# Far weight rooms moved by 64 bytes, and two short groups of small bfloat16 products in a tuned two-block transformer kernel

## The chip, the cores and the metric

The kernel runs on one core of a Trainium2 chip. The core has five engines that run their own instruction lists side by side: TensorE (PE, matrix products; its weight loads are listed apart as PEld), VectorE (DVE), ScalarE (ACT), GpSimd (POOL) and SyncE (SP, which here issues the DMAs). They share the on-chip memory SBUF; products land in PSUM. The metric is the time of one execution on the device in microseconds (us); lower is better. Three runs of the kernel before gave 1571.7, 1567.13 and 1571.4 us, median 1571.4.

## The reference

Two transformer blocks run one after the other on 256 tokens of width 1024, all in float32.

```python
# block 1
h = rms_norm(x, g_norm1) * (1 + scale1) + shift1
z = h @ w_in                                   # attention, index heads, pooling, gates
mixed = (g_attn * y_attn + g_pool * y_pool) @ w_out
x = x + gate1 * mixed
h2 = rms_norm(x, g_norm2) * (1 + scale2) + shift2
# experts: 16384 rows in u and v; 8 heads choose 16 each
s = einsum(h2 @ w_q, sub_keys); top_k twice     -> expert, gate
act = gelu(einsum('nd,ned->ne', h2, u[expert]))
x = x + gate2 * einsum('ne,ned->nd', gate * act, v[expert])
# block 2: recurrence and sparse attention, then the feed-forward
up = causal_dwconv(rms_norm(x, norm2_g) @ w_up, ffn_conv_w, ffn_conv_b)
gate, val = split(up, 2)
x = x + (gelu(gate) * val) @ w_down
```

The kernel does not gather the chosen experts. It multiplies with all of u (128 units), multiplies the result with a gate that is zero for experts that were not chosen, and multiplies that with all of v (128 units).

## The kernel before

**Units.** All large weights come as units of 128 partitions by 1024 float32 (8 blocks of 128x128). A unit is loaded by SP into `raw` (L116). ACT copies it rounded to `wh` (L178), and DVE, or POOL for some units of u, forms the rest `wl` = raw - wh (L179). The activations are split the same way (`h2` and its like: a high and a low part). `mm3` (L202) then multiplies a unit: 8 blocks wh x high, 8 blocks wh x low, 8 blocks wl x high, so 24 matmuls, each of 128x128 weights (a weight load of its own) against 256 columns. They add up in one PSUM tile `mm`.

**Rooms.** A unit's wh and wl lie in a room. The list `plan` (L152) says which units go to which rooms, repeating a string of letters. "w" are the two near rooms of pool `wp`, on the left of SBUF. "b" are two rooms in the tile `wpx` (L360) of pool `hot`, on the right; they serve w1 from unit 8, wup1 and wout1. "c" are two rooms of pool `wpu`, on the right, and serve u from unit 2 to 60 in the string "wwcc" (two units near, two far). "d" are three rooms in `spare` for v from unit 64, "e" one more near room from w2 on. The pool `hot` also holds, one after the other, the activations (`hot_acts`, L80: h2 for the experts, hb for w2) and the split gate products `pr` (L850). So in a matmul of u the moving activation lies in `hot` on the right, and the weight in a near or a far room.

**Order.** PE runs the units in the order of the code: w1, wup1, wout1, wpq (the queries of the experts), the first half of u (units 0 to 63, L825), the second half of u (L844) with 32 gate batches between its units, v (L869), w2, wup2, wout2, the feed-forward's first product (wff: 48 units in 24 steps `m` of two units) and second product (wdn: 24 units). During the first half of u, DVE works through the choice of the experts (`topk`, a generator of which a piece runs after most units). A gate batch (`gate_batch`, L784) builds masks on DVE and then runs 16 bfloat16 matmuls of 128x64 (L810) into a PSUM tile with the tag "x".

**Feed-forward.** For every step m (L1438) and i = 0, 1: a unit of wff, DVE scales the product to `zf` (L1445), ACT starts the convolution `cc` (L1448), DVE adds its two other taps (L1450, two instructions). After both: ACT applies gelu, POOL multiplies the halves (L1454), ACT rounds the product to `ffh` (L223), and DVE forms `ffl` (L224). The second product takes all 24 of ffh and ffl as moving operand: for each of 8 output tiles three units, of which the third needs ffh and ffl 16 to 23 (L1456).

`identb` is a bfloat16 unit matrix of 128x128, made at the start.

Of the kernel before, what the change touches and what calls it, by code (L numbers as in the profile page):

```python
# [7 lines left out]
F32 = mybir.dt.float32  # L8
F32R = mybir.dt.float32r
# [49 lines left out]
def tile_kernel(ctx: ExitStack, tc: tile.TileContext, I, out):  # L59
    nc = tc.nc  # L60
    V, S, G, T = nc.vector, nc.scalar, nc.gpsimd, nc.tensor
# [9 lines left out]
    px = ctx.enter_context(tc.tile_pool(name="px", bufs=2, space=PSUM))  # L71

    def pool(stack, name, bufs=1, **kw):
        return stack.enter_context(tc.tile_pool(name=name, bufs=bufs, reuse_waits="tile", **kw))
# [3 lines left out]
    hot = ctx.enter_context(tc.tile_pool(name="hot", bufs=1, reuse_waits="tile", side="right"))  # L78

    def hot_acts(name):  # L80
        t = hot.tile([128, 2, 8, 256], F32R, name=name, tag="hot")
        return t[:, 0], t[:, 1]


# [2 lines left out]
    x = const.tile([128, 8, 256], F32, name="x", tag="x")  # L87
# [16 lines left out]
    identb = const.tile([128, 128], BF, name="identb")  # L104
# [78 lines left out]
    def weights(name, i):  # L183

        if not ready:
            now[0] = None
            prefetch()
        now[0] = ready.pop(0)
        assert stream[now[0].pos] == (name, i)
        u = now[0]  # L190
        while len(ready) < 4 and prefetch():
            pass
        return u

    def mm3(ps, blocks, start=True, stop=True, by_block=False):

# [153 lines left out]
    with ExitStack() as ph:  # L350
# [6 lines left out]
        stp = ExitStack()  # L357
        psu = pool(stp, "psu", space=PSUM)
        wps = pool(stp, "wps", 6, side="left")
        wpx = hot.tile([128, 2, 2, 8, 128], F32R, name="wpx", tag="hot")  # L360
        rooms["a"] = Room(6, wps)
        rooms["b"] = Room(2, pairs=[(wpx[:, n, 0], wpx[:, n, 1]) for n in range(2)])
        sqrt_next()
# [3 lines left out]
        for i in range(2):  # L367
            pc = px.tile([128, 4, 128], F32, name="pc", tag="x")
            for k in range(4):
                T.matmul(pc[:, k], ident[0:8, 4 * i + k:4 * i + k + 1].to_broadcast([8, 128]), c8,  # L370
                         start=True, stop=True)
# [7 lines left out]
        h = (b1h.tile([128, 8, 258], F32R, name="hh"), b1h.tile([128, 8, 258], F32R, name="hl"))  # L379
# [16 lines left out]
        for m in range(8):  # L396
# [7 lines left out]
            n = b1w.tile([128, 256], F32, name="hn", bufs=3)  # L404
# [105 lines left out]
        for b in range(2):  # L510
            nk = 128 * (b + 1)
            sl = slice(b * 128, (b + 1) * 128)
            for gg in range(2):
                P = b1w.tile([128, 2, 2, 256], F32, name="P1")
                mx = b1w.tile([128, 3, 2, 2], F32, name="mx", bufs=3)
                for s in range(2):
                    base = 64 * s
                    pl = pa.tile([128, 2, 256], F32, name="pl", tag="a")
                    for c in range(2):
# [5 lines left out]
                        else:  # L525
                            tc.add_manual_dep(mm.ins, first.ins.name, no_sync(), reason="bank start")
                    T.matmul(pl[:, :, :nk], identb, bias[b][:, None, :].to_broadcast([128, 2, nk]),
                             start=False, stop=True, skip_group_check=True)
# [16 lines left out]
                for c in range(2):  # L545
                    po = px.tile([128, 128], F32, name="po", tag="x")
                    for s in range(2):
                        for k in range(b + 1):
                            T.matmul(po[64 * s:64 * s + 64], vt[:, k], pT[:, k, s, c],
                                     start=(k == 0), stop=(k == b))  # L550
# [106 lines left out]
        pxu = pool(upst, "pxu", 2, space=PSUM)  # L657
# [22 lines left out]
        for hd in range(8):  # L680
# [9 lines left out]
            for k in (2 * hd - 2, 2 * hd - 1) if 1 <= hd <= 4 else ():  # L690
                n = scr.tile([128, 256], F32, name="hn", bufs=2)
# [131 lines left out]
        rst = ExitStack()  # L823
        actA = None
        for i in range(64):  # L825
            if i == 0:
                pactA = pool(rst, "pactA", side="right")
                actA = [(0, pA0.tile([128, 24, 256], F32, name="actA0", tag="A0")),
                        (24, pactA.tile([128, 40, 256], F32, name="actA1"))]
                ust = ExitStack()  # L830
                rooms["c"] = Room(2, pool(ust, "wpu", 2, side="right"))
            u_unit(i, actA)
            if i == 0:
                late()
            if i % 5:
                next(tk, None)
# [10 lines left out]
                gate_batch(0, actA, n0, pxu if n0 % 16 else px)  # L847
                n0 += 8
        upst.close()
        pv_ = hot.tile([128, 8, 2, 256], F32R, name="pr", tag="hot")  # L850
        prs = [(pv_[:, 2 * n], pv_[:, 2 * n + 1]) for n in range(3)]
        vst = ExitStack()
        pv = pool(vst, "pv", side="right", space=PSUM)
# [15 lines left out]
        for i in range(128):  # L869
            u = weights("v", i)  # L870
            if i % 2 == 0:
                src = row(actA if i < 64 else actB, i % 64, 2)
                pr = prs[i // 2 % 3]
# [71 lines left out]
    with ExitStack() as ph:  # L945
# [131 lines left out]
        for kv in range(2):  # L1077
# [20 lines left out]
            for hf in range(2):  # L1098
                for l in range(8):
                    T.matmul(phd, cw[hf][:, l], cb[:, 8 * hf + l], start=(hf == 0 and l == 0),  # L1100
                             stop=(hf == 1 and l == 7))
# [332 lines left out]
    with ExitStack() as ph:  # L1434
        f1 = pool(ph, "f1", side="right")
        fw = pool(ph, "fw", 2, side="right")
        ff = (f1.tile([128, 24, 256], F32R, name="ffh"), f1.tile([128, 24, 256], F32R, name="ffl"))
        for m in range(24):  # L1438
            cv = []
            for i in range(2):  # L1440
                u = weights("wff", 2 * m + i)
                ps = pm4.tile([128, 256], F32, name="mm")
                mm3(ps, [(u, k, hf_, k) for k in range(8)], by_block=m == 0)
                z = fw.tile([128, 256], F32, name="zf", bufs=4)
                V.tensor_tensor(z, ps, r4, OP.mult)  # L1445
                ch = 24 * i + m
                cc = fw.tile([128, 256], F32, name=f"cc{i}")
                S.activation(cc, z, AF.Identity, bias=vcol("fb", ch), scale=vcol("fw", 96 + ch))  # L1448
                for j, d in ((1, 1), (0, 2)):
                    V.scalar_tensor_tensor(cc[:, d:], z[:, :256 - d], vcol("fw", 48 * j + ch),  # L1450
                                           cc[:, d:], op0=OP.mult, op1=OP.add)
                cv.append(cc)
            fact(cv[0], cv[0], AF.Gelu_apprx_tanh)
            G.tensor_tensor(cv[0], cv[0], cv[1], OP.mult)  # L1454
            split_act(ff, m, cv[0])
        for m in range(8):  # L1456
            ps = pm4.tile([128, 256], F32, name="mm")
            for j in range(3):
                u = weights("wdn", 3 * m + j)
                mm3(ps, [(u, k, ff, 8 * j + k) for k in range(8)], start=(j == 0), stop=(j == 2))  # L1460
            V.tensor_tensor(x2[:, m], ps, x2[:, m], OP.add)
            nc.sync.dma_start(out[:, m], x2[:, m])
# [112 lines left out]
```

## Time and profile before

| | |
|---|---|
| runs | 1571.7, 1567.13, 1571.4 us; median 1571.4 |
| profiled execution | 1572.43 us, of which the profile's span 1570.0 us |
| mean granted clock of TensorE | 0.989 of full speed |
| PE matmuls, busy | 1514.9 us (96%), 11758 matmuls |
| DVE, busy | 1286.6 us (82%) |
| ACT, busy | 831.3 us (53%) |
| POOL, busy | 213.6 us (14%) |
| HBM traffic | 279 MB read, 179 GB/s over the span |

The stages of the profiled execution, by the time at which PE works on them (us from the start of the span): w1, wup1, wout1 and wpq 57 to 217; first half of u 217 to 419; second half of u 419 to 609; v 610 to 980; w2 981 to 1277; wup2 and wout2 1277 to 1362; wff 1362 to 1499; wdn 1499 to 1567.

How to read it: matmuls of PE overlap. One that is listed with 0.28 us starts some 0.115 us after the one before it, so the pace is read from the starts, not from the durations. A row with "x16" stands for 16 instructions in a row of the same kind, its time running from the first start to the last end.

### The profile page before, as it was taken

The numbers are of one execution on the slowest core, as the hardware profiler recorded it, in microseconds if no ns is written. First come the engines' busy times: TensorE is split into PE (matmuls) and PEld (weight loads), VectorE is DVE, ScalarE is ACT, GpSimd is POOL, SyncE is SP. The second block draws the span as 40 slices with busy tenths as digits, with TensorE's granted clock in tenths as the row PEclk, the third lists the DMA queues.
The fourth block names the chain that finished last, engine by engine and source line by source line (L and its number), as shares of the span: only waits on it lengthen the run. The fifth ranks groups of instructions, "written<-read, shape, count | busy, mean of one in ns | idle before, by whom it ended". The sixth has DMA issues, their size and how long they took to land. (4 is left out here: it accounts for less than half of the span.)

```text
span 1570.0 us, 29771 instructions
## 1 busy us (share of the span) xinstructions
PE 1514.9 (96%) x11758; PEld 1404.7 (89%) x11758; DVE 1286.6 (82%) x2439; ACT 831.3 (53%) x1453; POOL 213.6 (14%) x156
## 2 busy tenths in 40 slices
PE   4999998999999999999999999988999999999999
PEld 3989998998999998888888888988888889999999
DVE  8899899993788987999966666978977766899963
ACT  3556564444444445444444444656777664666642
POOL 0100136896000000000000000026000000111100
PEclk9999999999999999999999999989999999999999
DMA  8778544655455555555566667453433235555663
GB/s 306 256 247 290 170 146 144 198 176 182 158 173 175 174 175 175 175 175 168 186 217 220 214 205 265 154 164 126 138 104 110 85 120 177 183 186 187 188 202 117
DMA packets 78203, 282.99 MB, mean 180 GB/s; under 512 B 8680, under 2 KB 9968, under 8 KB 77808
## 3 DMA queue, kind: packets, MB, share of 16 engines
q1 hardware_dynamic: 78064, 281.10, 54.8%
q8 instruction: 92, 1.51, 0.4%
q14 instruction: 47, 0.39, 0.1%
HBM read 278.97 MB, written 2.10 MB: 179 GB/s over the span
## 5 line engine op out<-in xcount | busy, mean ns | idle before, releaser
L178 ACT ACTIVATE wh<-raw 128x1024 fp32r<-128x1024 f32 x389 | 411.4, 1059 | 421.0 <-PE mm L202 212.8
L179 DVE TENSOR_TENSOR wl<-raw,wh 128x1024 fp32r<-128x1024 f32 x339 | 427.6, 1262 | 92.3 <-ACT wh L178 90.5
L202 PE MATMUL mm<-h,wh 128*128 128x256 f32 x2048 | 263.8, 282 | 0.0
L202 PEld LDWEIGHTS mm<-h,wh 128*128 128x128 f32 x2048 | 249.5, 191 | 0.2
L865 PE MATMUL vo<-spare,pr 128*128 128x512 f32 x768 | 176.0, 391 | 0.0
L865 PEld LDWEIGHTS vo<-spare,pr 128*128 128x128 f32 x768 | 144.2, 188 | 31.6
L202 PE MATMUL mm<-h,wl 128*128 128x256 f32 x1024 | 141.9, 282 | 8.3 <-DVE wl L179 8.3
L179 POOL TENSOR_TENSOR wl<-raw,wh 128x1024 fp32r<-128x1024 f32 x50 | 136.5, 2753 | 69.8 <-ACT wh L178 32.6
L268 POOL TENSOR_TENSOR r<-r,sq 128x256 f32<-128x256 f32 x18 | 13.7, 762 | 952.6 <-DVE hb L281 586.8
L202 PEld LDWEIGHTS mm<-h,wl 128*128 128x128 f32 x1024 | 129.9, 192 | 8.9 <-DVE wl L179 8.9
L202 PE MATMUL mm<-hb,wh 128*128 128x256 f32 x928 | 130.7, 287 | 0.6 <-ACT wh L178 0.2
L865 PE MATMUL vo<-wh,pr 128*128 128x512 f32 x512 | 130.8, 397 | 0.3 <-ACT pr L874 0.3
L179 DVE TENSOR_TENSOR spare<-raw,spare 128x1024 fp32r<-128x1024 f32 x64 | 78.4, 1226 | 56.3 <-ACT spare L178 56.0
L202 PEld LDWEIGHTS mm<-hb,wh 128*128 128x128 f32 x928 | 117.6, 192 | 3.7 <-issue 1.4
L178 ACT ACTIVATE spare<-raw 128x1024 fp32r<-128x1024 f32 x64 | 67.8, 1060 | 86.5 <-PE vo L865 85.8
L865 PEld LDWEIGHTS vo<-wh,pr 128*128 128x128 f32 x512 | 93.7, 188 | 19.0 <-ACT pr L874 0.4
L202 PE MATMUL mm<-hb,wl 128*128 128x256 f32 x464 | 69.3, 282 | 0.0
L865 PE MATMUL vo<-wl,pr 128*128 128x512 f32 x256 | 69.2, 392 | 0.0
L299 DVE SCALAR_TENSOR_TENSOR raw<-raw,cb 128x1024 f32<-128x1024 f32 x48 | 58.2, 1218 | 7.8 <-DMA raw<-in_wada_dram 7.8
L202 PEld LDWEIGHTS mm<-hb,wl 128*128 128x128 f32 x464 | 60.2, 190 | 0.3
L865 PEld LDWEIGHTS vo<-wl,pr 128*128 128x128 f32 x256 | 48.1, 188 | 10.7
L202 PE MATMUL mm<-hfh,wh 128*128 128x256 f32 x384 | 55.5, 281 | 0.0
(435 smaller groups left out, 2796.8 us busy)
## 6 DMA issues: line engine op xcount, KB each, us to landing
raw<-in_u_dram SPq DMA_DIRECT2D x128, 512.0 KB, 3.6
raw<-in_v_dram SPq DMA_DIRECT2D x128, 512.0 KB, 3.7
raw<-in_w_dram SPq DMA_DIRECT2D x86, 512.0 KB, 4.2
raw<-in_wada_dram SPq DMA_DIRECT2D x48, 512.0 KB, 5.2
raw<-in_wff_dram SPq DMA_DIRECT2D x48, 512.0 KB, 3.6
raw<-in_wup_dram SPq DMA_DIRECT2D x27, 512.0 KB, 3.9
raw<-in_wdn_dram SPq DMA_DIRECT2D x24, 512.0 KB, 3.5
raw<-in_wout_dram SPq DMA_DIRECT2D x16, 512.0 KB, 4.2
```

Source lines behind the costliest of these rows:

```text
L178: S.activation(u.h, t, AF.Copy)
L179: (G if n in on_pool and on_pool[n](i) else V).tensor_tensor(u.l, t, u.h.bitcast(F32), OP.subtract)
L202: T.matmul(ps, (u.l if wl else u.h)[:, s], a[al][:, k], start=start and n == 0, stop=stop and n == len(seq) - 1)
L268: eng.tensor_tensor(tot, tot, sq, OP.add)
L299: V.scalar_tensor_tensor(t, t, 1.0, cb, op0=OP.mult, op1=OP.mult, accum_out=a)
L865: T.matmul(vo[b][hf], pr[al][:, i % 2, b * 128:b * 128 + 128], (u.l if wl else u.h)[:, 4 * hf:4 * hf + 4], start=(i == 0 and n == 0), stop ...
```

## The change

It has two parts.

The first moves addresses. Every tile of the pool `hot` becomes 4128 instead of 4096 float32 long (128 bytes more in each partition; the added part is not used), the rooms "b" in `wpx` begin 16 floats (64 bytes) into their tile, and a tile of 16 floats (64 bytes) is put ahead of the rooms "c". What lies behind `hot` on the right moves by 128 bytes. The distance in bytes between a weight's address and its activation's, as the program lays the tiles out, is thus:

| weight room, stages | before, modulo 128 | after, modulo 128 | before, modulo 512 | after, modulo 512 |
|---|---|---|---|---|
| near rooms, u, w2, wout2, wff, wdn | 64 | 64 | 320 | 448 |
| far rooms "c", u 2 to 60 | 0 | 64 | 0 | 448 |
| rooms "b", wup1 and wout1 | 0 | 64 | 128 | 192 |
| near rooms, wup1 and wout1 | 64 | 64 | 448 | 64 |

The second part adds `pause(psum)`: 16 bfloat16 matmuls of identb (128x128) against 64 columns of identb, each with a weight load of its own, into a PSUM tile of the tag "x" that nobody reads. It stands in two places: ahead of unit 2 of u, and in the feed-forward ahead of the first unit of step m = 1.

```diff
@@ -78,7 +78,8 @@
     hot = ctx.enter_context(tc.tile_pool(name="hot", bufs=1, reuse_waits="tile", side="right"))
 
     def hot_acts(name):
-        t = hot.tile([128, 2, 8, 256], F32R, name=name, tag="hot")
+        t = hot.tile([128, 4128], F32R, name=name, tag="hot")[:, 0:4096].rearrange(
+            "p (h k n) -> p h k n", h=2, k=8)
         return t[:, 0], t[:, 1]
 
 
@@ -191,6 +192,12 @@
         while len(ready) < 4 and prefetch():
             pass
         return u
+
+    def pause(psum):
+
+        t = psum.tile([128, 8, 64], F32, name="pause", tag="x")
+        for n in range(16):
+            T.matmul(t[:, n % 8], identb, identb[:, 0:64], start=True, stop=True)
 
     def mm3(ps, blocks, start=True, stop=True, by_block=False):
 
@@ -357,7 +364,8 @@
         stp = ExitStack()
         psu = pool(stp, "psu", space=PSUM)
         wps = pool(stp, "wps", 6, side="left")
-        wpx = hot.tile([128, 2, 2, 8, 128], F32R, name="wpx", tag="hot")
+        wpx = hot.tile([128, 4128], F32R, name="wpx", tag="hot")[:, 16:4112].rearrange(
+            "p (n h k f) -> p n h k f", n=2, h=2, k=8)
         rooms["a"] = Room(6, wps)
         rooms["b"] = Room(2, pairs=[(wpx[:, n, 0], wpx[:, n, 1]) for n in range(2)])
         sqrt_next()
@@ -823,11 +831,14 @@
         rst = ExitStack()
         actA = None
         for i in range(64):
+            if i == 2:
+                pause(pxu)
             if i == 0:
                 pactA = pool(rst, "pactA", side="right")
                 actA = [(0, pA0.tile([128, 24, 256], F32, name="actA0", tag="A0")),
                         (24, pactA.tile([128, 40, 256], F32, name="actA1"))]
                 ust = ExitStack()
+                pool(ust, "wpu_pad", side="right").tile([128, 16], F32, name="wpu_pad")
                 rooms["c"] = Room(2, pool(ust, "wpu", 2, side="right"))
             u_unit(i, actA)
             if i == 0:
@@ -847,7 +858,8 @@
                 gate_batch(0, actA, n0, pxu if n0 % 16 else px)
                 n0 += 8
         upst.close()
-        pv_ = hot.tile([128, 8, 2, 256], F32R, name="pr", tag="hot")
+        pv_ = hot.tile([128, 4128], F32R, name="pr", tag="hot")[:, 0:4096].rearrange(
+            "p (m i n) -> p m i n", m=8, i=2)
         prs = [(pv_[:, 2 * n], pv_[:, 2 * n + 1]) for n in range(3)]
         vst = ExitStack()
         pv = pool(vst, "pv", side="right", space=PSUM)
@@ -1439,6 +1451,8 @@
             cv = []
             for i in range(2):
                 u = weights("wff", 2 * m + i)
+                if m == 1 and i == 0:
+                    pause(px)
                 ps = pm4.tile([128, 256], F32, name="mm")
                 mm3(ps, [(u, k, hf_, k) for k in range(8)], by_block=m == 0)
                 z = fw.tile([128, 256], F32, name="zf", bufs=4)
```

On DVE, ACT, POOL and SP the order of instructions is that of before; on PE it differs by the two pauses.

**First place**, PE before unit 2 of u. (`mm_...` are the PSUM tiles of one unit each, `h2` the activations of the experts, `pq` the scores of the chosen queries.) Before:

```order
L675 MATMUL pq_2759<-sub_2305,qh_2699 128x128 [waits Activation_49]
L675 MATMUL pq_2759<-sub_2305,qh_2699 128x128
L202 MATMUL mm_2764<-h2_2304,wh_2668 128x256 [waits DVE_49,PE_49]
L202 MATMUL mm_2764<-h2_2304,wh_2668 128x256 x15
L202 MATMUL mm_2764<-h2_2304,wl_2669 128x256 [waits Pool_49]
L202 MATMUL mm_2764<-h2_2304,wl_2669 128x256 x7
L202 MATMUL mm_2822<-h2_2304,wh_2724 128x256 [waits DVE_49]
L202 MATMUL mm_2822<-h2_2304,wh_2724 128x256 x15
L202 MATMUL mm_2822<-h2_2304,wl_2725 128x256 [waits Pool_49]
```

Before, the next unit follows at once. After, one pair of a weight load and a small matmul is shown, and 15 more like it are left out:

```order
L683 MATMUL pq_2763<-sub_2305,qh_2699 128x128
L209 MATMUL mm_2768<-h2_2304,wh_2668 128x256 [waits DVE_49,PE_49]
L209 MATMUL mm_2768<-h2_2304,wh_2668 128x256 x15
L209 MATMUL mm_2768<-h2_2304,wl_2669 128x256 [waits Pool_49]
L209 MATMUL mm_2768<-h2_2304,wl_2669 128x256 x7
L200 LDWEIGHTS identb_95
L200 MATMUL pause_2808<-identb_95 128x64
...
L209 MATMUL mm_2843<-h2_2304,wh_2728 128x256 [waits DVE_49]
L209 MATMUL mm_2843<-h2_2304,wh_2728 128x256 x15
L209 MATMUL mm_2843<-h2_2304,wl_2729 128x256 [waits Pool_49]
```

The 16 pairs of a weight load and a small matmul stand between unit 1 and unit 2, with no wait of their own; the units' own waits on DVE and POOL stay.

**Second place**, PE in the feed-forward between the two units of step 0 (by blocks, so wh, wl and both activation parts change from matmul to matmul) and the first unit of step 1. Before:

```order
L202 MATMUL mm_15965<-hfh_15610,wh_15869 128x256
L202 MATMUL mm_15965<-hfl_15611,wh_15869 128x256
L202 MATMUL mm_15965<-hfh_15610,wl_15870 128x256
L202 MATMUL mm_16006<-hfh_15610,wh_15924 128x256 x8
L202 MATMUL mm_16006<-hfl_15611,wh_15924 128x256 x8
L202 MATMUL mm_16006<-hfh_15610,wl_15925 128x256 x8
L202 MATMUL mm_16043<-hfh_15610,wh_15961 128x256 [waits Activation_49]
L202 MATMUL mm_16043<-hfh_15610,wh_15961 128x256 x7
```

Before, the row of units goes on into step 1 at its fourth row. After, again with one pair shown of 16:

```order
L209 MATMUL mm_15987<-hfh_15632,wh_15891 128x256
L209 MATMUL mm_15987<-hfl_15633,wh_15891 128x256
L209 MATMUL mm_15987<-hfh_15632,wl_15892 128x256
L200 LDWEIGHTS identb_95
L200 MATMUL pause_16028<-identb_95 128x64 [waits PE_49]
...
L209 MATMUL mm_16045<-hfh_15632,wh_15946 128x256 x8
L209 MATMUL mm_16045<-hfl_15633,wh_15946 128x256 x8
L209 MATMUL mm_16045<-hfh_15632,wl_15947 128x256 x8
L209 MATMUL mm_16082<-hfh_15632,wh_15983 128x256 [waits Activation_49]
L209 MATMUL mm_16082<-hfh_15632,wh_15983 128x256 x7
```

The pairs stand ahead of the first unit of step 1; the first of them waits for earlier work of PE itself on its PSUM tile.

## Rows read from the trace of the kernel before

**Rows 1.** The page: busy time, share of span and instructions of each engine.

```profile
PE 1514.9 (96%) x11758; PEld 1404.7 (89%) x11758; DVE 1286.6 (82%) x2439; ACT 831.3 (53%) x1453; POOL 213.6 (14%) x156
```

**Rows 2.** Windows: stretch, length, busy us by engine (instructions), PE clock, DMA share, GB/s.

```profile
130.00:160.00 30.00, 30.00 (x255) 30.00 (x254) 29.74 (x60) 16.51 (x26) 0.00 (x0) 1.00 0.84 293
217.00:360.00 143.00, 133.52 (x1095) 132.26 (x1094) 141.74 (x407) 64.09 (x104) 112.23 (x40) 0.97 0.49 159
360.00:419.00 59.00, 59.00 (x492) 59.00 (x492) 24.86 (x43) 28.21 (x43) 21.85 (x9) 0.98 0.58 188
419.00:609.00 190.00, 190.00 (x2027) 188.86 (x2026) 166.32 (x287) 83.87 (x127) 0.00 (x0) 1.00 0.54 175
1400.00:1490.00 90.00, 90.00 (x767) 90.00 (x766) 88.86 (x145) 60.59 (x97) 11.80 (x16) 1.00 0.60 188
1499.00:1530.00 31.00, 31.00 (x265) 31.00 (x264) 16.49 (x19) 12.78 (x15) 1.79 (x1) 1.00 0.64 200
```

**Rows 3.** Timeline of PE: start us, us, instructions; far units, then wout2.

```profile
231.84 2.08 PE L202 MATMUL mm<-h,wh 128*128 128x256 f32 x16
234.72 2.08 PE L202 MATMUL mm<-h,wh 128*128 128x256 f32 x16
...
1345.63 1.98 PE L202 MATMUL mm<-mix,wh 128*128 128x256 f32 x16
1348.36 1.98 PE L202 MATMUL mm<-mix,wh 128*128 128x256 f32 x16
```

**Rows 4.** Timeline of PE around one gate batch in the second half of u.

```profile
428.55 0.64 PE L810 MATMUL gt<-ab 128*128 128x64 f16 x16
429.03 2.08 PE L202 MATMUL mm<-h,wh 128*128 128x256 f32 x16
430.94 1.07 PE L202 MATMUL mm<-h,wl 128*128 128x256 f32 x8
431.85 1.98 PE L202 MATMUL mm<-h,wh 128*128 128x256 f32 x16
```

**Rows 5.** Waits between 217 and 420 us: total us, times, longest.

```profile
PE mm L202 <- DVE wl L179: 8.3, 3, 4.1
```

**Rows 6.** Timeline at the second of these waits, DVE and PE.

```profile
355.86 3.40 DVE L179 TENSOR_TENSOR wl<-raw,wh 128x1024 fp32r<-128x1024 f32 x1
...
359.31 2.08 PE L202 MATMUL mm<-h,wl 128*128 128x256 f32 x8 [3.74 <-DVE wl L179]
```

**Rows 7.** Windows right behind that wait, columns as in rows 2.

```profile
359.20:362.20 3.00, 2.89 (x13) 2.89 (x14) 0.06 (x1) 0.00 (x0) 0.00 (x0) 0.50 0.65 179
362.20:366.00 3.80, 3.80 (x34) 3.80 (x33) 1.23 (x1) 2.57 (x4) 0.67 (x1) 0.98 1.00 400
```

**Rows 8.** Timeline of PE early in wff, step m = 0.

```profile
1364.36 0.70 PE L273 MATMUL ss<-r,ones 128*128 128x256 f32 x2 [0.54 <-POOL r L268]
```

**Rows 9.** DVE between 1400 and 1490 us by line: count, busy us, mean ns, idle before.

```profile
L179 DVE TENSOR_TENSOR wl<-raw,wh 128x1024 fp32r<-128x1024 f32 x32 | 47.2, 1477 | 0.0
L1450 DVE SCALAR_TENSOR_TENSOR cc<-zf,vec,cc 128x255 f32<-128x255 f32 x33 | 15.7, 475 | 0.0
L1450 DVE SCALAR_TENSOR_TENSOR cc<-zf,vec,cc 128x254 f32<-128x254 f32 x32 | 15.5, 483 | 1.1
L1445 DVE TENSOR_TENSOR zf<-mm,r 128x256 f32<-128x256 f32 x32 | 13.4, 418 | 0.0
L224 DVE TENSOR_TENSOR ffl<-cc,ffh 128x256 fp32r<-128x256 f32 x16 | 6.6, 412 | 0.0
```

**Rows 10.** Timeline where wff ends and wdn begins.

```profile
1499.74 1.11 PE L202 MATMUL mm<-ffl,wh 128*128 128x256 f32 x8
...
1503.83 0.42 ACT L223 ACTIVATE ffh<-cc 128x256 fp32r<-128x256 f32 x1 [1.89 <-POOL cc L1454]
1504.28 0.42 DVE L224 TENSOR_TENSOR ffl<-cc,ffh 128x256 fp32r<-128x256 f32 x1 [1.08 <-ACT ffh L223]
...
1504.46 1.10 PE L202 MATMUL mm<-ffh,wh 128*128 128x256 f32 x8
```

## The prediction

> **What bounds the kernel now.** I read the page's engine totals first: PE is busy for 1514.9 of 1570.0 us, DVE for 1286.6 [rows 1]. A share over the whole span says little, so the second view is the windows by stage [rows 2]. The reader should see three kinds of stage there. In the second half of u, and from 360 to 419, PE is busy all the time and DVE is not: what a matmul takes is what the stage takes. In the first half of u up to 360, DVE has 141.74 of 143 us and PE waits. In the first product of the feed-forward both are full: 90.00 and 88.86 of 90 us.
>
> The third view is the timeline of PE, read for starts. The same instruction, 128x256 float32, runs at three paces. A unit of 24 in a far room takes 234.72 - 231.84 = 2.88 us, 120 ns each; a unit of wout2 takes 1348.36 - 1345.63 = 2.73 us, 113.5 ns each [rows 3]; in the feed-forward 40 matmuls take 1504.46 - 1499.74 = 4.72 us, 118 ns each [rows 10]. I call them 120, 118 and 113. At full clock all three occur, so the clock is not the reason. Two things go with the pace. One is the room: far rooms, where the distance of weight and activation is 0 modulo 128 bytes, are at 120 throughout. The other is history: near rooms keep 113 or 118 for hundreds of matmuls and change when something breaks the row of units. A gate batch of 16 small matmuls is such a break. It takes 429.03 - 428.55 = 0.48 us, the next 16 matmuls take 1.91 us instead of 1.81, and then 8 take 0.91, which is 113 [rows 4]. The whole second half of u has 32 batches and 2027 - 32 x 16 = 1515 large matmuls in 190.0 us: (190.0 - 32 x 0.58) / 1515 = 113.2 [rows 2]. In the feed-forward the pace falls to 118 behind a short wait at 1364 [rows 8], and 118 it stays.
>
> The Trainium skill speaks against a part of this. Its page "TensorE: Matmul & The Clock Gate", "Step-by-step: what each phase is for", says that PE has two independent read ports into SBUF and that loading the next weights takes no bandwidth from the running matmul. By that, an address could not matter, and moving the rooms would be worth nothing. The trace does not agree: 2.88 against 2.73 us for the same 24 matmuls at full clock.
>
> **Pauses, their own price.** By the gate batch one pause is 0.48 + 0.10 = 0.58 us of PE. It copies the same form (16 matmuls of 64 columns, each with its weights), so I take that value; the lower bound is 0.48. The second pause's wait is for PE's own earlier work and costs nothing that I can see. Nothing else is added to any queue.
>
> **First half of u, to 360 us.** Pause 1 stands at about 226 us. PE waits here for DVE's wl three times, 8.3 us in all [rows 5], the last time 3.74 us at 359.31 [rows 6]. DVE is in the topk without a gap. So the 0.58 us of the pause, and all that far rooms at 113 or 118 give back before 359, only move the length of that wait. If the cover were gone, the pause would cost its 0.58. What can move the end is DVE itself: the wl that PE waits for took 3.40 us against a mean of 1.48 [rows 6, 9], because POOL makes another one beside it. Other meetings of the two may make this part about 2 us shorter or longer; I take 0.
>
> **360 to 419 us.** PE is full, DVE has 24.86 of 59 us [rows 2]. The first 2.2 us run at half clock behind the wait: 13 matmuls in 3.0 us where 34 fit into 3.8 at the full clock [rows 7], so about 1.0 us is the clock's. The rest is (59.0 - 1.0) / 492 = 118. Half of the units are far ones. If the move only makes far rooms like near ones at 118, the gain is 246 x 2 ns = 0.5 us; if all run at 113, it is 492 x 4.5 = 2.2 us. Pause 1 lies more than 130 us ahead, and two waits of some 4 us stand between, behind which near rooms of before came out at 118 and not at 113. I take 1.0; the ends are 0 and 2.2.
>
> **Rooms b, 130 to 217 us.** Some 400 matmuls of wup1 and wout1 run at 30.00/255 = 118 ns. DVE is as full as PE there, 29.74 of 30 us [rows 2], so of 400 x 4.5 = 1.8 us little can arrive. I take 0.3, between 0 and 1.8.
>
> **Feed-forward.** From pause 2 to the end PE has 46 + 24 units, 1680 matmuls. At 113 instead of 118 that is 1680 x 4.5 = 7.6 us; less 0.58 for the pause it would be 7.0, if PE set the time. It doesn't alone. For one step of two units PE needs 48 x 0.1175 = 5.64 us now and 48 x 0.1133 = 5.44 then; DVE's work is 88.86 / 16 = 5.55, two wl, two zf, four cc and one ffl [rows 9]. With PE faster, DVE is late next. PE can live on the units that DVE has ready, so the wait need not come in each step; it comes at the latest at the joint. The last ffh is written from 1503.83 to 1504.25 by ACT, behind POOL and DVE [rows 10]; PE first uses it as the eighth matmul of the row that begins at 1504.46, at 1505.28. The slack is 1.0 us. So this half gains 1.0, up to 2.4 if DVE also loses its 1.1 us of gaps [rows 9]. PE would arrive there 1159 x 4.5 ns - 0.58 = 4.6 us early and wait 3.6. Behind the like wait at 359 the clock was 0.50 for 3 us [rows 7]: 12 matmuls too few, 1.4 us. After it, 521 matmuls are left with DVE half idle, 16.49 of 31 us [rows 2]: 521 x 4.5 = 2.3 us if the pace is 113 after the wait, 0 if it is 118. I take 1.0 + 2.3 - 1.4 = 1.9, between -0.4 (no more than the slack, clock paid, pace 118) and 7.0.
>
> **Everything else.** The second half of u is at 113 already, v has other operands (128x512), and w2 is mostly at 113. All their distances stay 64 modulo 128, so I take 0; what it costs if 128 is not the period is rival three.
>
> **Sum.** 0 + 1.0 + 0.3 + 1.9 = 3.2 us. The profiled execution took 1572.4 us (span 1570.0): 1569.2. The median of the runs is 1.0 us below that execution, so against runs I say 1568.2 us, 0.2% under 1571.4. A difference under 0.3%, 4.7 us, can hardly be told from none here: 1566.7 to 1576.1 counts as the same.
>
> **Rival one: the pace does not change.** A pause of constant weights in the near rooms may not do what a gate batch does; behind other breaks, as at 1364, 118 came out [rows 8]. Then the feed-forward costs 0.6 and the far rooms give 0.5: 1572.4 + 0.1 - 1.0 = 1571.5. For it: the feed-forward has hfl and ffh operands from other tiles than u. Against it: all batches of the second half of u ended at 113. By the page's rule of the two ports the far rooms would give nothing either, and the time would be 1571.4 + 0.6 = 1572.0 with a pause that does nothing. Chance 0.17 for both.
>
> **Rival two: the feed-forward is bound by PE after all.** DVE's wl of 1.48 us is a mean that takes in meetings with POOL, which can lengthen one to 3.40 [rows 6, 9]. If faster PE moves the meetings, DVE's 5.55 falls and PE's 7.0 us arrive nearly whole, with 2.2 from 360 to 419 and 0.3 from rooms b: 1572.4 - 9.5 - 1.0 = 1561.9. Against it: DVE's idle is 1.1 us in 90, and the joint of the two products has one chain through POOL. Chance 0.19.
>
> **Rival three: slower, the good pace is lost.** The longer tiles in `hot` change the distance of every near room from 320 to 448 modulo 512. If what matters repeats only every 256 or 512 bytes, the 113 pace of before could go. Some 2700 matmuls run at it, 1515 in the second half of u and the rest in w2 and wout2; at 118 they take 2700 x 4.5 = 12.2 us more, and the feed-forward pays 0.6 for its pause: 1572.4 + 12.8 - 1.0 = 1584. It decides as soon as more than a third of them are lost. For it: the one stage of before whose near rooms stand at 448, wup1 and wout1, is at 118 throughout [rows 2]. Against it: every second pair of units there lies in rooms at 120, and no break of small matmuls comes. Chance 0.17.
>
> **How the numbers follow.** My forecast has 0.47, its own range is 1564 to 1573; a third of it, 0.15, ends under 1566.7. Faster: 0.15 + 0.19 = 0.34. Same: 0.32 + 0.16 = 0.48. Slower: 0.17 + 0.01 = 0.18. The range goes to 1560 for the second rival with its 2 us of DVE luck, and to 1579 for a third rival in which only half of the pace is lost; some 0.17 is left out.
>
> **What would show it.** Far units from 231 us at 2.72 to 2.83 us instead of 2.88 show the first part right; 2.88 would be the page's rule. Eight matmuls in 0.91 us behind pause 2 show the second. A wait of PE for ffh or wl between 1460 and 1505, with a lower clock behind it, shows the limit by DVE. A unit of 2.73 us becoming 2.83 in the second half of u would make me wrong on the slow side; v at another pace than before would make me wrong on either.

## The result, and the profile after

The changed kernel takes 1586.8 us (median of four runs, 1585.8 to 1587.1) where the kernel before takes 1571.55 beside it: a ratio of 1.0095, 95% interval 1.0072 to 1.0118. It is slower by 15 us, 1%, and outside the range of 1560 to 1579. The profiled execution has a span of 1584.7 us.

The page of the changed kernel, engine totals, answers to [rows 1]: PE is busy 14.6 us longer, about as much as the span grew (14.7). DVE and POOL are busy for less, ACT for 3.4 us more.

```profile
PE 1529.5 (97%) x11790; PEld 1412.2 (89%) x11790; DVE 1277.7 (81%) x2439; ACT 834.7 (53%) x1453; POOL 209.6 (13%) x156
```

To see where, I took the start of the same matmul in both traces at the borders of the stages. The differences add up to 14.7 us. The second half of u, v, wup2 and wout2 together lost 13.8 of it:

| stretch (us of before) | before, us | after minus before, us |
|---|---|---|
| up to 57 | 57.1 | +1.1 |
| 57 to 85, w1 | 28.0 | +4.1 |
| 85 to 217 | 131.8 | -1.1 |
| 217 to 360, first half of u | 143.1 | -1.5 |
| 360 to 419 | 59.0 | -1.3 |
| 419 to 609, second half of u | 190.0 | +6.3 |
| 612 to 979, v | 367.1 | +6.0 |
| 985 to 1100, w2 | 115.0 | -1.5 |
| 1100 to 1277, w2 | 177.0 | +0.6 |
| 1277 to 1369, wup2, wout2 (+1.5), start of wff with pause 2 (+0.6) | 92.0 | +2.1 |
| 1369 to the end, wff and wdn | 197.5 | 0.0 |

Windows of the changed kernel over the second half of u, v and the second part of w2 (columns as in [rows 2]):

```profile
420.50:616.70 196.20, 196.20 (x2027) 194.75 (x2025) 166.35 (x287) 83.89 (x127) 0.00 (x0) 1.00 0.54 170
619.60:992.70 373.10, 373.10 (x2011) 298.47 (x2011) 290.55 (x423) 171.10 (x195) 0.00 (x0) 1.00 0.62 197
1112.00:1289.70 177.70, 174.84 (x1373) 156.53 (x1372) 135.66 (x291) 128.44 (x350) 0.00 (x0) 1.00 0.33 106
```

The same windows over v and the second part of w2 in the kernel before:

```profile
612.00:979.00 367.00, 367.00 (x2011) 298.07 (x2010) 289.98 (x423) 171.43 (x195) 0.00 (x0) 1.00 0.62 201
1100.00:1277.00 177.00, 172.72 (x1372) 154.01 (x1370) 135.68 (x290) 128.42 (x350) 0.00 (x0) 1.00 0.32 106
```

The same 2027 matmuls of the second half of u took 190.00 us before [rows 2] and take 196.20 at full clock; the same 2011 of v took 367.00 and take 373.10. In both stages PE was full before and after, so every nanosecond of a matmul arrives. PE does not wait there: the matmuls themselves follow each other more slowly. A gate batch shows how. The timeline of PE in the changed kernel answers to [rows 4] (the line of `mm3` is L209 there):

```profile
436.44 0.64 PE L818 MATMUL gt<-ab 128*128 128x64 f16 x16
436.91 2.13 PE L209 MATMUL mm<-h,wh 128*128 128x256 f32 x16
438.88 1.10 PE L209 MATMUL mm<-h,wl 128*128 128x256 f32 x8
439.82 2.05 PE L209 MATMUL mm<-h,wh 128*128 128x256 f32 x16
```

Behind the batch the first 16 matmuls take 1.97 us and the next 8 take 0.94, which is 118 ns each, where [rows 4] had 1.91 and 0.91, which is 113. In the kernel before, the first batch of the second half of u finds 118 and leaves 113, and the other 31 keep it. In the changed kernel all 32 find 118 and leave it.

The two pauses cost what was expected, and bring nothing here. The timeline of PE at the first one:

```profile
229.74 1.10 PE L209 MATMUL mm<-h,wl 128*128 128x256 f32 x8
230.69 0.64 PE L200 MATMUL pause<-identb 128*128 128x64 bf16 x16
231.16 2.13 PE L209 MATMUL mm<-h,wh 128*128 128x256 f32 x16
233.13 1.10 PE L209 MATMUL mm<-h,wl 128*128 128x256 f32 x8
234.08 1.10 PE L209 MATMUL mm<-h,wh 128*128 128x256 f32 x8
```

The pace is 118 ahead of it (230.69 - 229.74 = 0.95 us for 8) and behind it (234.08 - 233.13 = 0.95). In the feed-forward 8 matmuls take 0.94 behind the second one, to the end. The far rooms did get better: from the pause to 256 us, and from 365 to 420, all units run at 118, none at 120.

One part of the table has another cause. In w1 the clock fell to 0.50 in this execution (windows of the changed kernel, then of the kernel before):

```profile
67.00:72.00 5.00, 5.00 (x26) 3.54 (x26) 4.32 (x13) 1.51 (x6) 0.62 (x4) 0.63 0.65 196
72.00:77.00 5.00, 5.00 (x20) 3.90 (x21) 2.84 (x15) 1.84 (x4) 0.00 (x0) 0.50 0.57 196
```

```profile
67.00:72.00 5.00, 5.00 (x33) 3.69 (x32) 4.71 (x16) 2.24 (x9) 0.16 (x2) 1.00 0.61 206
```

That is the +4.1. It came in some of the profiled executions of the experiments and not in others, with the addresses of before as with those of the change (in the run with eight pauses in the feed-forward, at the addresses of the change, it did not come), and I count it to neither. Whether the change brings it more often is open: the four runs of the changed kernel lie within 1.3 us of each other, so it may have come in all of them. The small gains in the table, 5.4 us in all, and the losses up to 85, 5.2 us, nearly cancel.

### The profile page after: what moved, and what is told of

The parts are those of the page before. It is cut to its first block, busy times and chain, and to the rows that moved or that the text cites. A ratio compares the mean times of both kernels' runs of the same rounds, so it can differ in the third digit from the quotient of the medians.

```text
span 1584.7 us, 29834 instructions
## 1 busy us (share of the span) xinstructions
PE 1529.5 (97%) x11790; PEld 1412.2 (89%) x11790; DVE 1277.7 (81%) x2439; ACT 834.7 (53%) x1453; POOL 209.6 (13%) x156
## 5 line engine op out<-in xcount | busy, mean ns | idle before, releaser
L209 PE MATMUL mm<-h,wh 128*128 128x256 f32 x2048 | 265.7, 281 | 0.0
L209 PEld LDWEIGHTS mm<-h,wh 128*128 128x128 f32 x2048 | 250.8, 188 | 0.2
L877 PE MATMUL vo<-spare,pr 128*128 128x512 f32 x768 | 179.4, 396 | 0.0
L209 PE MATMUL mm<-h,wl 128*128 128x256 f32 x1024 | 142.2, 281 | 8.6 <-DVE wl L180 8.6
L209 PEld LDWEIGHTS mm<-h,wl 128*128 128x128 f32 x1024 | 130.1, 188 | 9.2 <-DVE wl L180 9.2
L209 PE MATMUL mm<-hb,wh 128*128 128x256 f32 x928 | 131.8, 287 | 0.4 <-ACT wh L179 0.2
L209 PEld LDWEIGHTS mm<-hb,wh 128*128 128x128 f32 x928 | 118.5, 190 | 3.5 <-issue 1.4
L209 PE MATMUL mm<-hb,wl 128*128 128x256 f32 x464 | 70.2, 283 | 0.0
L209 PEld LDWEIGHTS mm<-hb,wl 128*128 128x128 f32 x464 | 61.3, 189 | 0.1
L209 PE MATMUL mm<-hfh,wh 128*128 128x256 f32 x384 | 55.6, 280 | 0.0
```

Of the source, the lines that this page charges most:

```text
L209: T.matmul(ps, (u.l if wl else u.h)[:, s], a[al][:, k], start=start and n == 0, stop=stop and n == len(seq) - 1)
L877: T.matmul(vo[b][hf], pr[al][:, i % 2, b * 128:b * 128 + 128], (u.l if wl else u.h)[:, 4 * hf:4 * hf + 4], start=(i == 0 and n == 0), stop ...
```

## Experiments

The distance is that of a unit's room from the activation's tile that it meets, as the program lays them out: address of the room less address of the tile. Modulo 256 bytes the near rooms stand at 64 before and at 192 after; below, "at 64" and "at 192" mean that. In v the roles on PE are exchanged (`pr` in hot is the weight, the unit moves). There, too, 64 and 192 are counted from the tile in hot to the room; from the moving operand to the weight they would be 192 before and 64 after.

**Theory and rivals.** Theory: the 128 bytes that were added to `hot` moved the near rooms to a distance at which breaks of the row leave 118. Rivals: the pauses leave PE at 118; or it is the place of the tiles in SBUF and not their distance.

**The pauses alone**, all addresses as before:

```diff
+            if i == 2:
+                pause(pxu)
...
+                if m == 1 and i == 0:
+                    pause(px)
```

> The kernel before with the two pauses alone, all addresses as before. Distance theory (the longer tiles moved every near room from 320 to 448 bytes modulo 512, and at 448 the row of units does not come back to the 113 ns pace): second half of u in 190 us again, v in 370, the time within 2 us of before, 1570 to 1573. Pause theory (the pauses leave PE at 118 from the start of u on): second half of u near 196 us, the time near 1583 to 1587. In the feed-forward this run also says whether a pause gives 113 at a distance of 320: 2.72 us a unit if it does, 2.83 if not.

Measured: 1574.4 us, ratio to before 1.0013 (0.9985 to 1.0041; all ratios are to runs of the kernel before beside it). Windows over the second half of u and v:

```profile
424.20:614.20 190.00, 190.00 (x2027) 188.86 (x2025) 166.35 (x287) 84.00 (x127) 0.00 (x0) 1.00 0.56 175
617.20:984.20 367.00, 367.00 (x2011) 298.12 (x2010) 289.73 (x423) 171.57 (x195) 0.00 (x0) 1.00 0.63 201
```

Both stages as before: the pauses are not the cause. In the feed-forward the start left 118, and the pause did not change it.

**The moved addresses alone**, the two calls of `pause` taken out of the changed kernel:

```diff
-            if i == 2:
-                pause(pxu)
...
-                if m == 1 and i == 0:
-                    pause(px)
```

> The changed kernel without its two pauses, addresses all as changed. Distance theory: second half of u near 196 us with 118 ns behind every gate batch, v near 376, the time 1584 to 1587. Pause theory: 190 and 370 us, the time 1570 to 1573.

Measured: 1587.4 us, ratio 1.0115 (1.0088 to 1.0142): the whole loss.

```profile
419.40:615.60 196.20, 196.20 (x2026) 194.75 (x2025) 166.36 (x287) 83.89 (x127) 0.00 (x0) 1.00 0.55 170
618.60:991.70 373.10, 373.10 (x2012) 298.49 (x2011) 290.56 (x423) 171.52 (x195) 0.00 (x0) 1.00 0.62 197
```

Against the strict form of my theory, the feed-forward of this execution ran at 113 at a distance of 192, after the wait at its start (8 matmuls from 1383.86 to 1384.76 us). So 113 exists at 192 too; it is the gate batches that don't lead there.

**The change without two older fillers.** The fillers of 96 bytes on the left and 32 on the right go; near rooms are at 64 modulo 256 again, `hot` stays longer, the far rooms of u stay at 192:

```diff
-    const.tile([128, 24], F32, name="near_pad")
-    far_pad = ctx.enter_context(tc.tile_pool(name="far_pad", bufs=1, side="right"))
-    far_pad.tile([128, 8], F32, name="far_pad")
```

> The changed kernel without the two older fillers at the ends of SBUF (96 bytes on the left, 32 on the right), so that the near rooms stand again at 320 modulo 512 from their activations while the tiles of hot stay longer and the far rooms of u stay at 448. Distance theory: second half of u 190 us, v 370, the time 1569 to 1573. If it is the place of the tiles itself and not the distance: near 1586.

Measured: 1567.1 us, ratio 0.998 (0.996 to 1.0001).

```profile
418.70:608.70 190.00, 190.00 (x2027) 188.83 (x2025) 166.34 (x287) 84.02 (x127) 0.00 (x0) 1.00 0.56 175
611.60:978.60 367.00, 367.00 (x2011) 298.07 (x2010) 289.68 (x423) 171.42 (x195) 0.00 (x0) 1.00 0.64 200
```

Near rooms and activations both stand 96 bytes from where they stood before, and both stages are as before: it is the distance, not the place. Its first half of u says a second thing. Near rooms (64) and far rooms (192) follow each other in pairs there. The rows are a far unit, two near ones and a far one, all at 2.72 us:

```profile
374.09 1.98 PE L206 MATMUL mm<-h,wh 128*128 128x256 f32 x16
376.81 1.98 PE L206 MATMUL mm<-h,wh 128*128 128x256 f32 x16
379.53 1.98 PE L206 MATMUL mm<-h,wh 128*128 128x256 f32 x16
382.25 1.98 PE L206 MATMUL mm<-h,wh 128*128 128x256 f32 x16
```

A row at 113 goes on through rooms at 192. Through far rooms at 0 it does not [rows 3]. So 64 and 192 can both hold 113; which of the two it is says what a break leaves.

**The period.** The same fillers taken out of the kernel before: near rooms at 192 modulo 512, which is 192 modulo 256 as in the changed kernel, but another value modulo 512. (The diff is that of the run above, on the kernel before.)

> The kernel before without the two older fillers at the ends of SBUF, so that near rooms stand at 192 modulo 512 from their activations (192 modulo 256, as the 448 of the changed kernel; before had 320, 64 modulo 256), far rooms of u at 0 as before. If the distance counts modulo 256: second half of u near 196 us, the time near 1586. If it counts modulo 512, or only modulo 128: 190 us and near 1571. What v does (its distances become 320 and 64) says the same a second time: 370 us, or 376.

Measured: 1581.4 us in one run. The windows of the same two stages:

```profile
415.30:611.50 196.20, 196.20 (x2026) 194.76 (x2024) 166.35 (x287) 83.85 (x127) 0.00 (x0) 1.00 0.54 170
614.30:987.40 373.10, 373.10 (x2011) 298.48 (x2011) 290.66 (x423) 171.27 (x195) 0.00 (x0) 1.00 0.62 197
```

196.20 and 373.10 again, to the tenth: the distance counts modulo 256. Its first gate batch found 113 and left 118, the reverse of the kernel before (8 matmuls in 0.91 us ahead of it, in 0.94 behind it):

```profile
414.40 1.07 PE L199 MATMUL mm<-h,wl 128*128 128x256 f32 x8
415.31 0.64 PE L807 MATMUL gt<-ab 128*128 128x64 f16 x16
...
417.76 1.10 PE L199 MATMUL mm<-h,wl 128*128 128x256 f32 x8
418.70 0.64 PE L807 MATMUL gt<-ab 128*128 128x64 f16 x16
```

The first half of u of this run shows that 192 is not simply the worse distance. Its far rooms stand at 0, as in the kernel before. The rows are a far unit and the two near ones behind it, first in this run, then in the kernel before:

```profile
234.63 2.08 PE L199 MATMUL mm<-h,wh 128*128 128x256 f32 x16
237.51 1.98 PE L199 MATMUL mm<-h,wh 128*128 128x256 f32 x16
240.23 1.98 PE L199 MATMUL mm<-h,wh 128*128 128x256 f32 x16
```

```profile
237.59 2.05 PE L202 MATMUL mm<-h,wh 128*128 128x256 f32 x16
240.42 2.05 PE L202 MATMUL mm<-h,wh 128*128 128x256 f32 x16
```

Behind a far unit at 120 the near ones at 192 run at 113 (240.23 - 237.51 = 2.72 us a unit), the near ones at 64 at 118 (2.83), at twelve of twelve such places at full clock in either run. So the two distances answer the two kinds of break in opposite ways: a gate batch leaves 113 at 64 and 118 at 192, a room at 0 leaves 118 at 64 and 113 at 192. In the changed kernel the far rooms stand at 192 as well, so this way to 113 is gone too.

**Far rooms at 64 as well.** 192 bytes ahead of the far rooms of u instead of 64, `hot` as before, both pauses:

```diff
+                pool(ust, "wpu_pad", side="right").tile([128, 48], F32, name="wpu_pad")
```

> The kernel before with the two pauses and 192 bytes ahead of the far rooms of u, so that near and far rooms both stand at 320 modulo 512; the tiles of hot are as before. Distance theory: units of 2.72 us in the first half of u from pause 1 to 256 us and again behind 361 us if the pace survives the waits, far units no longer 2.88; second half of u 190 us; the time 1567 to 1571. Pause theory: near 1584.

Measured: 1566.0 us, ratio 0.9969 (0.9951 to 0.9987), faster than both kernels. Far units take 2.72 us from pause 1 on wherever PE does not wait, and 360 to 419 is 3.4 us shorter. In this execution the feed-forward ran at 113 already ahead of its pause, and gained 4.9 us up to 1499. The timeline of its end, to be read beside [rows 10]:

```profile
1495.60 1.55 POOL L1465 TENSOR_TENSOR cc<-cc,cc 128x256 f32<-128x256 f32 x1 [4.88 <-DVE cc L1461]
1497.17 0.42 ACT L229 ACTIVATE ffh<-cc 128x256 fp32r<-128x256 f32 x1 [2.18 <-POOL cc L1465]
...
1497.64 0.38 PE L208 MATMUL mm<-ffh,wh 128*128 128x256 f32 x1 [3.34 <-ACT ffh L229]
```

PE waits 3.34 us for the last ffh, and behind the wait the granted clock is half (0.50):

```profile
1499.00:1502.00 3.00, 3.00 (x16) 3.00 (x16) 2.09 (x3) 1.06 (x1) 0.00 (x0) 0.50 0.56 160
```

Of the 4.9 us, 3.3 go at the joint; 0.7 come back in wdn, after the clock is paid.

**The same without pauses, and with one of them.**

> The kernel before with nothing but 192 bytes ahead of the far rooms of u (near and far both at 320 modulo 512), no pauses. If the pauses are neutral in the row of units: u from 361 to 419 us faster by about 3 us as with them, no 0.6 us for a pause on the path, the feed-forward at 113 or at 118 by what its wait at the start leaves; time 1564 to 1570. If the pauses were what kept 113 there: u from 361 to 419 within 1 us of before, time 1570 to 1573.

Measured: 1573.9 us, ratio 0.9999 (0.9974 to 1.0023), spread 1563.9 to 1577.0. In its profile the feed-forward ran at 118, and 217 to 360 took 3.5 us longer than in the profile with both pauses.

Only the pause in the feed-forward:

> 192 bytes ahead of the far rooms of u, and of the two pauses only the one in the feed-forward. If it was the pause in the feed-forward that made the run with both pauses faster than the one with none (1566.0 against 1573.9 us, each beside its own runs of before): 1565 to 1568. If it was the pause in u, by the time at which ACT, DVE and POOL meet there: 1571 to 1575.

Measured: 1568.3 us, ratio 0.9965 (0.9933 to 0.9997).

Only the pause in u:

> The same with only the pause in u. If the pause in u was it: 217 to 361 us some 4 us shorter than without it, the time 1565 to 1568. If it was the other: 1571 to 1575.

Measured: 1568.6 us, ratio 0.9973 (0.9952 to 0.9995). In the five profiles with the pause in u and far rooms at 64 (one of each kernel), 217 to 360 is 1.9 to 4.1 us shorter than before; in the three without it 0.6 to 1.4 longer. That fits a gain by the pause in u. But this stretch is also 1.5 and 1.4 us shorter without any pause in the run of the moved addresses alone and in that of the period, and the times of the last two runs, 1568.3 and 1568.6, do not tell the pauses apart. Which pause is worth how much, and by what way, stays open.

**Does a pause set the pace?** In the kernel before, pauses ahead of the units 40 to 59 of u, and none elsewhere:

```diff
+            if 40 <= i < 60:
+                pause(pxu)
```

> The kernel before with a pause ahead of each of the units 40 to 59 of u, none elsewhere; far rooms at 0, near at 320 modulo 512. If a pause sets the pace as a gate batch does: the first near unit behind a pause that follows a near unit at 118 runs at 113. If a pause keeps the pace that it finds: it stays at 118, and far units at 120 are followed by whatever the change of room leaves, as without pauses. The time is no question here (up to 11 us of pauses).

The timeline of PE (time 1582.6 us with twenty pauses):

```profile
368.75 0.99 PE L208 MATMUL mm<-h,wl 128*128 128x256 f32 x7
369.58 0.64 PE L199 MATMUL pause<-identb 128*128 128x64 bf16 x16
370.06 2.06 PE L208 MATMUL mm<-h,wh 128*128 128x256 f32 x16
371.95 1.07 PE L208 MATMUL mm<-h,wl 128*128 128x256 f32 x8
372.87 0.64 PE L199 MATMUL pause<-identb 128*128 128x64 bf16 x16
```

From a near unit at 118 (7 in 0.83 us) to the next near unit at 113 (8 in 0.92, with the start of the next pause): so at four of four such places. Far units at 0 stayed at 120.

Then in the feed-forward, ahead of steps 1 to 20, addresses of before:

```diff
+                if 1 <= m < 21 and i == 0:
+                    pause(px)
```

> The kernel before with a pause ahead of the first unit of the steps 1 to 20 of the feed-forward and none elsewhere; distance 64 modulo 256. If a pause brings the row of units to 113 at this distance, as the gate batches do: whatever the pace at the start, 113 behind the first or the second pause and from there on. If it keeps the pace that it finds: the pace of the start to the end, 118 where it starts at 118. Twenty pauses cost 11.6 us of PE.

```profile
1365.90 0.64 PE L199 MATMUL pause<-identb 128*128 128x64 bf16 x16
...
1367.40 1.11 PE L208 MATMUL mm<-hfl,wh 128*128 128x256 f32 x8
1368.34 1.11 PE L208 MATMUL mm<-hfh,wl 128*128 128x256 f32 x8
...
1372.12 0.64 PE L199 MATMUL pause<-identb 128*128 128x64 bf16 x16
...
1373.59 1.07 PE L208 MATMUL mm<-hfl,wh 128*128 128x256 f32 x8
1374.49 1.07 PE L208 MATMUL mm<-hfh,wl 128*128 128x256 f32 x8
```

The pause at step 1 found 118 and left 118 (0.94 us for 8), the one at step 2 left 113 (0.90), and 18 more kept it. The time is 1573.4 us in one run. So a pause at 64 can set 113, but need not: over all profiles at 64 it stood between a near unit at 118 and another near unit ten times, left 113 five times and 118 five. Step 1 is where the change puts it; there it left 118 in all three cases. At step 2 it left 113 here and 118 in the last run below.

And at 192: the changed kernel with pauses ahead of steps 1 to 8.

> The changed kernel with its pause in u and pauses ahead of steps 1 to 8 of the feed-forward instead of step 1 alone; near rooms at 192 modulo 256. If the distance decides: 118 (2.83 us a unit) behind every one of them, even should the feed-forward start at 113, time near 1591. If only the place of the first pause was bad: 113 from step 2 on.

```profile
1380.22 1.10 PE L209 MATMUL mm<-hfl,wh 128*128 128x256 f32 x8
1381.16 1.10 PE L209 MATMUL mm<-hfh,wl 128*128 128x256 f32 x8
...
1384.93 0.64 PE L200 MATMUL pause<-identb 128*128 128x64 bf16 x16
```

118 (0.94 us for 8) behind all eight, and behind the one in u; time 1586.7 in one run (w1 was at full clock in it). With the gate batches of the second half of u in the four kernels at 192, 128 in all, no break of small bfloat16 products at 192 led from 118 to 113. So in the change two things go with the 118 of the feed-forward: the distance, and a place of the pause that left 118 at 64 as well.

**The pause one step later, and a lighter DVE.** 192 bytes ahead of the far rooms, pause in u, the other one at step 2:

> 192 bytes ahead of the far rooms of u, pause in u, and the pause of the feed-forward at step 2 instead of step 1; near rooms at 64 modulo 256. If the place decides: 113 from step 2 on in every execution, DVE then sets the end of the first product and PE waits some 3.5 us at the joint; time 1564 to 1567, with less spread than with the pause at step 1. If the first product's pace is worth nothing because of DVE: no different from the pause at step 1, 1566 to 1569.

Measured: 1569.3 us, ratio 0.9968 (0.9938 to 0.9999). The feed-forward of the profile was at 113 before the pause came, so the place wasn't put to the test; PE waited 3.3 us at the joint, and ran at 118 behind it.

With `ffl` on POOL for 22 of the 24 steps, first without pauses, then with the two of the change, then with the one at step 2:

```diff
-            split_act(ff, m, cv[0])
+            split_act(ff, m, cv[0], G if m < 22 else None)
```

> As the run with 192 bytes ahead of the far rooms and no pauses, and the low part of the feed-forward's product made by POOL instead of DVE for the first 22 of 24 steps (0.41 us of DVE a step). If DVE is what holds the feed-forward at the joint: where the pace is 113, the wait of PE at the joint falls from 3.4 us to under 1 and the time is some 3 us less than without it. If meetings of POOL and DVE cost as much: no gain, or 1 to 3 us more.

> 192 bytes ahead of the far rooms, both pauses, and the low part of the feed-forward's product on POOL for 22 of 24 steps. If DVE holds the feed-forward: where it runs at 113 the wait of PE at the joint of the two products falls from 3.4 us to under 1.5, the time 1562 to 1565. If the meetings of POOL and DVE cost as much: 1565 to 1568 and the wait as long.

> The same, with the low part of the feed-forward's product on POOL for 22 of 24 steps, so that DVE has 0.41 us less a step. If DVE holds the joint: PE's wait there falls from about 3.5 us to under 1.5 and the time by 2 to 3 us. If POOL's second instruction delays DVE as much as it relieves it: wait and time unchanged or worse.

Measured: 1571.2, 1569.1 and 1571.2 us, ratios 0.9989 (0.9966 to 1.0012), 0.9977 (0.9949 to 1.0006) and 0.9978 (0.9946 to 1.0011): no better than DVE. All three profiles had the feed-forward at 118, so what it would do at 113 was not seen (in the last one both pauses found 118 and left 118). Why it is worth little can be seen even so, in the groups of POOL and DVE of the last of them from 1395 to 1485 us (busy us, mean ns, idle before):

```profile
L230 POOL TENSOR_TENSOR ffl<-cc,ffh 128x256 fp32r<-128x256 f32 x16 | 18.4, 1150 | 8.5 <-ACT ffh L229 8.5
```

```profile
L1461 DVE SCALAR_TENSOR_TENSOR cc<-zf,vec,cc 128x255 f32<-128x255 f32 x32 | 22.3, 697 | 0.0
```

DVE lost the 6.6 us of ffl [rows 9], and its first tap grew from 475 to 697 ns, 15.7 to 22.3 us: the same 6.6 us. The 16 taps that overlap an ffl on POOL take 914 ns on average, the 16 others 480. DVE is busy for 88.91 of the 90 us, against 88.86 before.

## Why the prediction was wrong

**The step that failed** is "everything else": all distances stay 64 modulo 128, so I took 0 for the second half of u, v and w2. The period is 256 bytes, and two of these stages lost 6.3 and 6.0 us. I had taken the period from far rooms against near ones, 0 against 64 modulo 128, though the rows of before could not tell 128 from 256: the near rooms that ran at 113 all stood at 320 modulo 512. The stage that could have warned, near rooms at 448 that run at 118 [rows 2], I named and gave 0.17.

**Rival three was the case**: I gave it a loss of 12.2 us and a time of 1584, and 1586.8 came. That its sum is so near is partly luck, since its parts were sized less well. The second half of u lost 6.3 where 1515 x 4.5 = 6.8 stood. w2 and wout2 had some 5.4 in the bill and lost 1.5 in wup2 and wout2, half in each, and 0.6 in the second part of w2. In that part PE's busy time rose by 2.1 us, 172.72 to 174.84, but the window only by 0.7, so most of it went into time in which PE had been idle. In the first part of w2 the -1.5 goes with a stretch at half clock (1038 to 1052) that was shorter, 7 us instead of 14, in this execution. v was missing from the bill: I had set it aside for its other operands (128x512). There `pr` in hot is the weight and the unit moves; its pace went from 229 ns to 233, and in every run v was slow where the second half of u was slow. As weight less moving operand its distance is 192 where it is fast and 64 where it is slow, the reverse of u: what the two have in common is the distance from the tile in hot to the room.

**The price of a pause** was right: 0.58 forecast, 0.56 measured at 1362 to 1369. What it does was put too simply. I took a gate batch for its model, which led from 118 to 113 in all five profiles at 64 in which the first one found 118; a pause of constant operands did so in five cases of ten. In the feed-forward rival one was the case.

**217 to 360** came out as bounded: 0 with ends of 2 us, and -1.5 was measured. Over the profiles it went from -4.1 (far rooms at 64, pauses, ffl on POOL) to +2.1 (pauses alone; the run with twenty pauses left aside), wider than the 2 us that I gave it. The stage ends when DVE's chain ends; what moves that was not tried by itself.

**360 to 419**: -1.0 forecast, -1.3 measured, with all units at 118, and most of that is luck. In the changed kernel no half clock stands at 359 any more: the wait came earlier. The run of the pauses alone, whose far rooms stay at 0, has -1.0 here by that alone, so far rooms at 118 instead of 120 gave some 0.3, against the 0.5 that I had for this case. The upper end of 2.2 was too small for the same reason: at 113 the runs gave 2.9 and 3.4. One reading of mine was wrong too: behind the first of the two waits of before, near units ran at 113 (267.35 to 270.08, 2.73 us a unit), not at 118.

**Rooms b**: -0.3 forecast, -0.2 measured between 130 and 217, and for the reason given. In wup1 all units ran at 113, 21.78 us instead of 22.70, and a new wait of 1.1 us for DVE behind it (PE for `mixl`, in wout1) took the gain. In the kernel before, rooms b ran at 118 to 119 there, not at the 120 that rival three gives them; they stand at 128 modulo 256, not at 0.

**The feed-forward** brought none of its 1.9 us, because 113 did not come. Where it did come (192 bytes, both pauses), the sum held: -4.91 up to 1499, +3.34 at the joint where I had a wait of 3.6, -0.66 behind it with half clock for 3 us as at 359, +0.43 for the start with the pause: -1.80. The pause was not what brought it: 113 stood ahead of it. The second rival, PE alone, was wrong: in all six profiles in which the first product ran at 113 with at most one pause, PE waited 3.3 to 3.8 us at the joint for the last ffh, which stands behind POOL and DVE.

**The page's rule.** The Trainium skill, "TensorE: Matmul & The Clock Gate", "Step-by-step: what each phase is for", gives TensorE two independent read ports, one for weights and one for moving data. The trace does not agree that they are independent in time: the distance of the two operands alone moved v from 367.0 to 373.1 us at full clock, in each of the four kernels at 192. Where they meet, no run here shows.

## What to carry to other kernels

Where PE is full, compare the starts of equal matmuls before anything else: 113 and 120 ns for one instruction differ by 6%. If the distance of weight and activation is tuned, treat it as something that every longer tile in the same pool changes, and keep it fixed modulo 256 bytes; a filler that lines up one pair of rooms must not move the others. No distance is best by itself: look at which breaks stand in the row and what each leaves. A gain of PE's pace in a stage where a second engine is 99% busy arrives only up to the next joint.

## What the runs showed of the hardware

The same 128x256 float32 matmul has paces that hold for hundreds of instructions and survive 16 small ones in between. A distance of 64 or 192 modulo 256 between the two operands can hold 113 ns; far rooms at 0 ran at 120 throughout in u. In the second half of u the gate batches left 113 in all thirteen profiles at 64 and 118 in all four at 192. Rooms at 0 did the opposite: the near unit behind them ran at 118 at 64 and at 113 at 192. Waits can switch the pace either way: the one at the start of the feed-forward left 113 in one profile of four at 192 and in five of thirteen at 64. The runs of the kernel before lie between 1565 and 1586 us. The pace behind waits, and a stretch of half clock in w1 that comes and goes (4 us), may be two of the reasons; no run here singles them out.
